# Two modulation products moved behind the experts, one into the end of the RWKV loop, and key factors formed in place

## The chip, the cores and the metric

The kernel runs on one core of a Trainium2 chip. The metric is the device time of one execution in microseconds (us), the median of several runs. TensorE is called PE in the profile (its weight loads PEld), VectorE DVE, ScalarE ACT, GpSimd POOL; SP only issues DMAs.

## The reference, cut to what matters

The block has two layers over 512 latent and 256 context tokens of width 1024 (six tiles of 128 tokens; tiles 0 and 1 are the context). Layer 0 mixes tokens with RWKV-7 heads and S5 groups, layer 1 with latent attention (MLA); each layer ends in a mixture of experts. Both layers are modulated by a vector made from the conditioning:

```
m_l = jnp.split((silu_c @ mod_w[layer] + mod_b[layer])[:, None, :], 6, axis=-1)
m_c = jnp.split(silu_cc @ mod_w[layer] + mod_b[layer], 6, axis=-1)
a_l = modulate(rmsnorm(h_lat, norm1_g[layer]), m_l[0], m_l[1])
...                                   # the layer's mixer gives o_l
h_lat = h_lat + m_l[2] * o_l
f_l = modulate(rmsnorm(h_lat, norm2_g[layer]), m_l[3], m_l[4])
h_lat = h_lat + m_l[5] * moe_ffn(f_l, ...)
```

The six vectors of a layer are one product of 1024 by 6144, 25.2 MB of weights for two rows of input.

## The kernel before

**Modulation.** The product is cut into parts `mod_part(l, q)`: part q = 0 gives shift and scale of the first norm, 1 the first gate and the second shift, 2 the second scale and gate. A part loads 8.39 MB as 16 DMAs of 512 KB on SP (tile `mw`, 128 partitions by 4 by 256 columns, three buffers); each load feeds four products of 256 columns, one in each group of 32 columns of the array. They count as eight PE instructions in the profile, since fp32 takes two passes. They add into `psmod`; DVE adds the bias (`mb`) and SP writes the result to DRAM (`mods`), from where the norms read it.

**Stages.** In the front, layer 0's input projection runs (`pwi`, `pkb`, `ptv`, then `pws` of `w_in_s5`) with all three parts of layer 0 between its pieces. Then comes the loop of `rwkv`: s runs over 0 to 5, and each s makes one step of both scan directions. Stage a (`rwkv_stage_a`) forms decays and key factors on DVE, ACT and POOL (`plo`, `sg`, `ev`, `KB`, `wseg`) two steps ahead. Stage b solves a triangular system one step ahead: DVE makes `X`, SP stores it (`xo`) and loads it as blocks (`D`), and PE with DVE and ACT turns it into an inverse (`pd`, `W`, `G`, `pt`, `Tb`). The steps use it (`pU`, `VU`, `pY`, `pZ`, then the state `Z`). `rwkv_out` makes a token tile's output (`yo`), for tiles 0 and 1 in s = 3, for two more in each of s = 4 and 5. `MODN` puts layer 1's three parts into s = 3, 4 and 5. After the loop come the output projection (`po`) and the experts of layer 0, 768 tokens, whose results (`yo`) go to a DRAM buffer (`yb`).

**MLA stage.** POOL gathers the experts' rows (`cy<-yb`), DVE and POOL combine them into `h`, and SP stores the four latent tiles (`hbuf`). Each tile is normed and transposed (`ntt`), projected (`pmi`), normed and transposed again (`pmt`), and expanded (`pv`). Then attention starts (`pqp`, then `pqn`, `st`).

**What sets the order.** A scheduler simulates the kernel at build time and writes every engine's instructions in one order; on the chip each engine takes them strictly in that order, and a buffer's next user waits for its last reader.

Of the kernel before, what the change touches and what calls it, by code (L numbers as in the profile page):

```python
# [21 lines left out]
OP = mybir.AluOpType  # L22
# [25 lines left out]
MODN = {3: (0,), 4: (1,), 5: (2,)}  # L48
# [39 lines left out]
class Block:  # L88
# [35 lines left out]
    def cond(self, tp):  # L124
        nc, i = self.nc, self.i
        cr = tp.tile([16, 128], F32, name="cr")
        nc.sync.dma_start(cr[0:8, :], i["c"].rearrange("b (k p) -> (b k) p", p=128))
        nc.sync.dma_start(cr[8:16, :], i["c_ctx"].rearrange("(k p) -> k p", p=128))
        cs = tp.tile([16, 128], F32, name="csil")
        nc.scalar.activation(cs, cr, AF.Tanh, scale=0.5)  # L130
        nc.vector.tensor_scalar(cs, cs, 0.5, 0.5, op0=OP.mult, op1=OP.add)
        nc.vector.tensor_tensor(cs, cs, cr, OP.mult)
        pt = self.psum("tp", "pt_c", 2)
        nc.tensor.transpose(pt[:, :16], cs, self.ident[:16, :16])
        self.cst = self.c0.tile([128, 8, 32], F32, name="cst")
        nc.gpsimd.memset(self.cst, 0.0)
        nc.vector.tensor_copy(self.cst[:, :, 0:2], pt[:, :16].rearrange("p (v k) -> p k v", v=2))

    def mod_part(self, l, q, wpool, spool, tag="mod"):
# [18 lines left out]
        for k in range(8):  # L158
            for h in range(2):
                wt = wpool.tile([128, 4, 256], F32, name=f"mw{l}{q}{k}{h}", tag="mw")  # L160
                w = i["mod_w"][l, k * 128:(k + 1) * 128, q * 2048:q * 2048 + 2048].rearrange("p (j c) -> p j c", j=4)
                last = nc.sync.dma_start(wt, w[:, :, 256 * h:256 * h + 256])
                for j in range(4):
                    nc.tensor.matmul(ps[32 * j:32 * j + 32, 256 * h:256 * h + 256], self.cst[:, k, :], wt[:, j],  # L164
                                     start=(k == 0 and h == 0), stop=(k == 7), skip_group_check=True)
# [311 lines left out]
    def rwkv_stage_a(self, s, sp, wp, tag=("gr",), bufs=2):  # L477
# [3 lines left out]
        for z in range(2):  # L481
# [952 lines left out]
    def row_psum(self, rows, name):  # L1434

        out = [self.psum("cb", f"{name}{hf}", 2) for hf in range(2)]
# [178 lines left out]
    def mla_values(self, t):  # L1615

        nc = self.nc
        ts = slice(t * 128, t * 128 + 128)
        for hh in range(2):
            hs = slice(hh * 8, hh * 8 + 8)  # L1620
            ps = self.psum("ca", f"pv{t}{hh}", 2)
            self.mm3(ps, (self.kvT[0][:, ts], self.kvT[1][:, ts]), [x[:, hs, :].rearrange("p h c -> p (h c)") for x in self.kw],
                     True, True)
            dst, src = self.vv[:, t, hs], ps.rearrange("p (h c) -> p h c", h=8)
            if hh:
                nc.vector.tensor_copy(dst, src)
            else:
                nc.scalar.activation(dst, src, AF.Copy)

    def mla_down(self, aT, t, sp):  # L1630
# [12 lines left out]
        pt = self.psum("cb", f"pmt{t}", 2)  # L1643
        if t >= 2:
            r = self.rstd_of(sp, ps[:, 0:256], f"mq{t}", 256)
            qn = sp.tile([128, 256], F32, name=f"qn{t}", tag="qn", bufs=2)
            nc.vector.scalar_tensor_tensor(qn, ps[:, 0:256], r, self.qnb, op0=OP.mult, op1=OP.mult)
            for k in range(2):
                nc.tensor.transpose(pt[:, k * 128:(k + 1) * 128], qn[:, k::2], self.ident)
        r = self.rstd_of(sp, ps[:, 256:384], f"mk{t}", 128)  # L1650
        kn = sp.tile([128, 128], F32, name=f"kn{t}", tag="kn", bufs=2)
        nc.vector.scalar_tensor_tensor(kn, ps[:, 256:384], r, self.kvb, op0=OP.mult, op1=OP.mult)
# [175 lines left out]
    def front(self, qd, es):  # L1828
# [5 lines left out]
        with ExitStack() as e0:  # L1834
# [33 lines left out]
            self.mod_part(0, 2, mp, ms)  # L1868
# [17 lines left out]
    def rwkv(self, es, s5d, rwd):  # L1886
# [25 lines left out]
        for s in range(6):  # L1912
# [47 lines left out]
    def build(self):  # L1960
# [7 lines left out]
        with ExitStack() as es:  # L1968
# [10 lines left out]
            with ExitStack() as ec:  # L1979
# [7 lines left out]
                 lambda: self.mla_weights(self.pool("mlaw", 1, es=mes, side="right")))  # L1987
        with ExitStack() as e0:
# [9 lines left out]
            with ExitStack() as e1:  # L1998
# [5 lines left out]
                for v in (1, 0):  # L2004
                    for hf, ps in enumerate(self.row_psum(self.g2r[:, v], f"g2c{v}")):
                        nc.scalar.activation(g2c[v][:, hf * 512:hf * 512 + 512], ps, AF.Copy)
                self.mla_split(wp)

                def normed(t):
                    h = hts[t]  # L2010
                    self.combine(self.fetch(0, t, xp, 2), h, g2c[int(t < 2)],
# [3 lines left out]
                    r = self.rstd_of(xp, h, f"n1{t}")  # L2015
# [151 lines left out]
```

## Time and profile before

| | us |
|---|---|
| median of three runs | 1959.4 |
| lowest, highest | 1953.17, 1964.0 |
| profiled execution, its own time | 1948.41 |
| its span in the trace | 1946.6 |
| PE busy | 1563.9 (80%) |
| DVE busy | 1218.9 (63%) |
| ACT, POOL busy | 774.2, 701.3 |

The profiled execution took 1.8 us more than its span, and 11 us less than the median. Its mean granted clock of PE is 0.88 of full speed. Stages in the trace: front to about 330 us, loop to 874, output projection and experts to 1268, MLA stage before attention to 1378.

### The profile page before, as it was taken

The numbers are of one execution on the slowest core, as the hardware profiler recorded it, in microseconds if no ns is written. First come the engines' busy times: TensorE is split into PE (matmuls) and PEld (weight loads), VectorE is DVE, ScalarE is ACT, GpSimd is POOL, SyncE is SP. The second block draws the span as 40 slices with busy tenths as digits, with TensorE's granted clock in tenths as the row PEclk, the third lists the DMA queues.
The fourth block names the chain that finished last, engine by engine and source line by source line (L and its number), as shares of the span: only waits on it lengthen the run. The fifth ranks groups of instructions, "written<-read, shape, count | busy, mean of one in ns | idle before, by whom it ended". The sixth has DMA issues, their size and how long they took to land. (4 is left out here: it accounts for less than half of the span.)

```text
span 1946.6 us, 32507 instructions
## 1 busy us (share of the span) xinstructions
PE 1563.9 (80%) x12531; PEld 1126.9 (58%) x12531; DVE 1218.9 (63%) x2385; ACT 774.2 (40%) x1434; POOL 701.3 (36%) x700
## 2 busy tenths in 40 slices
PE   5698898558687789649698999949699998789993
PEld 2376767447576655337575666638455556666662
DVE  4799933884866867243754654475678854575544
ACT  4222324334543523132413555433556543335542
POOL 0476802441423414102514233451143353324432
PEclk8688999678898869679899999969799998899997
DMA  8754587723233268743605999852000009349965
GB/s 257 213 174 157 164 275 218 218 60 109 62 88 103 72 223 258 241 170 128 246 33 188 389 354 367 328 175 65 1 1 1 1 0 367 110 168 370 377 230 184
DMA packets 222854, 347.65 MB, mean 179 GB/s; under 512 B 49538, under 2 KB 170296, under 8 KB 207784
## 3 DMA queue, kind: packets, MB, share of 16 engines
q1 hardware_dynamic: 206784, 294.71, 45.4%
q0 software_dynamic: 10080, 44.04, 6.3%
q10 hardware_dynamic: 5832, 6.78, 1.1%
q8 instruction: 100, 1.64, 0.3%
q14 instruction: 58, 0.48, 0.1%
HBM read 279.02 MB, written 66.46 MB: 177 GB/s over the span
## 5 line engine op out<-in xcount | busy, mean ns | idle before, releaser
L164 PE MATMUL psmod<-mw,cst 128*32 128x256 f32 x768 | 83.8, 491 | 43.5 <-DMA mw<-in_mod_w_dram 39.2
L191 PE MATMUL pwi<-aT,wih 128*128 128x256 f32 (+1 forms) x224 | 81.7, 367 | 14.4 <-DVE q L334 7.2
L192 PE MATMUL pwi<-aT,wih 128*128 128x256 f32 (+1 forms) x224 | 81.9, 367 | 0.0
L193 PE MATMUL pwi<-aT,wil 128*128 128x512 f32 (+1 forms) x224 | 81.2, 364 | 0.0
L1784 ACT ACTIVATE P<-st 128x512 f32<-128x512 f32 x96 | 56.9, 596 | 48.7 <-PE st L1782 44.7
L1797 POOL TENSOR_TENSOR sum<-sum,P 128x512 f32<-128x512 f32 x48 | 63.6, 1348 | 27.8 <-ACT P L1784 27.6
L1112 PE MATMUL s5y<-s5tq,s5H 128*96 128x128 f32 x256 | 50.6, 333 | 27.3 <-POOL s5H L1104 15.1
L1415 POOL DMA_INDIRECT xg<-fbuf,rk x36 | 37.8, 1051 | 92.9 <-PE ptx L231 52.3
L572 PE MATMUL pg<-PQ,KB 64*128 64x128 f32 x384 | 54.1, 318 | 18.7 <-ACT ta L501 10.4
L1098 POOL TENSOR_TENSOR s5t<-s5G,s5tq 128x384 f32<-128x384 f32 x16 | 18.0, 1123 | 141.5 <-DVE s5G L1095 121.3
L185 ACT ACTIVATE xT<-ptx 128x512 fp32r<-128x512 f32 x72 | 41.2, 596 | 66.1 <-PE ptx L231 65.0
L164 PEld LDWEIGHTS psmod<-mw,cst 128*32 128x32 f32 x768 | 20.3, 124 | 77.4 <-DMA mw<-in_mod_w_dram 55.7
L186 DVE TENSOR_TENSOR xT<-ptx,xT 128x512 fp32r<-128x512 f32 x72 | 48.2, 688 | 23.1 <-ACT xT L185 22.2
L572 PEld LDWEIGHTS pg<-PQ,KB 64*128 64x128 f32 x384 | 44.1, 211 | 31.2 <-ACT ta L501 10.7
L191 PEld LDWEIGHTS pwi<-aT,wih 128*128 128x128 f32 x224 | 46.2, 208 | 22.3 <-issue 11.4
L1112 PEld LDWEIGHTS s5y<-s5tq,s5H 128*96 128x96 f32 x256 | 37.8, 198 | 35.9 <-POOL s5H L1104 16.8
L1795 POOL TENSOR_TENSOR sum<-P,P 128x512 f32<-128x512 f32 x16 | 20.5, 1300 | 105.3 <-ACT P L1784 105.2
L231 PEld LDWEIGHTS ptx<-ident,xg 128*128 128x128 f32 x288 | 40.6, 192 | 26.6 <-issue 21.0
L1788 PE MATMUL po<-P,vv 128*64 128x512 f32 x192 | 54.3, 617 | 1.1 <-ACT P L1784 1.1
L685 PE MATMUL pU<-Z,PQ 128*64 128x128 f32 x192 | 30.3, 331 | 27.9 <-ACT Z L677 27.7
L231 PE MATMUL ptx<-ident,xg 128*128 128x128 f32 x288 | 42.9, 285 | 10.9 <-issue 7.0
L192 PEld LDWEIGHTS pwi<-aT,wih 128*128 128x128 f32 x224 | 46.1, 206 | 7.8 <-issue 3.1
(1569 smaller groups left out, 5161.0 us busy)
## 6 DMA issues: line engine op xcount, KB each, us to landing
mw<-in_mod_w_dram SPq DMA_DIRECT2D x96, 512.0 KB
yb<-yo SPq DMA_DIRECT2D x36, 512.0 KB
s5tq<-s5t SPq DMA_DIRECT2D x16, 960.0 KB
yb<-zrow SPq DMA_DIRECT2D x16, 512.0 KB
wi<-in_hy_w_in_dram SPq DMA_DIRECT2D x14, 512.0 KB
rk<-qbuf SPq DMA_DIRECT2D x12, 512.0 KB
fbuf<-f SPq DMA_DIRECT2D x10, 512.0 KB
s5t<-s5CP SPq DMA_DIRECT2D x4, 1152.0 KB
```

Source lines behind the costliest of these rows:

```text
L164: nc.tensor.matmul(ps[32 * j:32 * j + 32, 256 * h:256 * h + 256], self.cst[:, k, :], wt[:, j], start=(k == 0 and h == 0), stop=(k == 7), s ...
L185: nc.scalar.activation(hi, src, AF.Copy)
L186: nc.vector.tensor_tensor(lo, src, hi.bitcast(F32), OP.subtract)
L191: nc.tensor.matmul(out, lh, rh, start=start, stop=False, **kw)
L192: nc.tensor.matmul(out, lh, rl, start=False, stop=False, **kw)
L193: nc.tensor.matmul(out, ll, rh, start=False, stop=stop, **kw)
L231: nc.tensor.transpose(pt[:, k * 128:(k + 1) * 128], a[:, h * 4 + k::8], self.ident)
L572: nc.tensor.matmul(pg[hp][:, m], KB[rs, m, ps2], PQ[rs, m, ps2], start=True, stop=True, skip_group_check=True)
L1112: nc.tensor.matmul(out, H[:, g, d, k, h0:h0 + 96], CP[:, k, d, i0:i0 + 8, :].rearrange("p a b -> p (a b)"), start=False, stop=(d == 1 and ...
L1784: ex = nc.scalar.activation(P, st, AF.Exp, scale=SCALE)
L1788: mm = nc.tensor.matmul(po[64 * x:64 * x + 64], vv[:, kt, h0 + x, :], P, start=(kt == 0), stop=(kt == 5), skip_group_check=True)
L1797: nc.gpsimd.tensor_tensor(sums[x], sums[x], P, OP.add)
```

## The change

`MODN` now holds part (0, 2) in s = 3 and part (1, 0) in s = 4. Parts (1, 1) and (1, 2) stand in the MLA stage behind the experts of layer 0, with 128 columns for each load: 64 loads of 256 KB in four buffers, and half as long products. They have their own accumulator bank `md`, for which `pv`, `pmt` and `g2c` share the three buffers of tag `cb`. `rwkv_out` of tiles 0 and 1 moves to s = 4, behind that step's own tiles. The key factors are written straight to their strided places in `KB`, so `ev` is no longer written a second time in stage a. Three squares for norms are written to tiles that exist anyway (left out below).

```
-MODN = {3: (0,), 4: (1,), 5: (2,)}
+MODN = {3: ((0, 2),), 4: ((1, 0),)}
...
-    def mod_part(self, l, q, wpool, spool, tag="mod"):
+    def mod_part(self, l, q, wpool, spool, tag="mod", parts=2, bufs=None):
...
-            for h in range(2):
-                wt = wpool.tile([128, 4, 256], F32, name=f"mw{l}{q}{k}{h}", tag="mw")
+            for h in range(parts):
+                n = 512 // parts
+                wt = wpool.tile([128, 4, n], F32, name=f"mw{l}{q}{k}{h}", tag="mw", bufs=bufs)
...
-            t1 = ev
             for m in range(4):
-                nc.scalar.activation(t1[:, m, :], ta[:, m, :], AF.Identity, scale=self.hka[:, 0, m:m + 1],
+                nc.scalar.activation(ends(KB)[:, m], spl(ta)[:, m], AF.Identity, scale=self.hka[:, 0, m:m + 1],
                                      bias=self.hka[:, 1, m:m + 1])
-            nc.gpsimd.tensor_tensor(t1, t1, k, OP.mult)
-            nc.vector.tensor_tensor(ends(KB), spl(t1), e3, OP.mult)
+            nc.gpsimd.tensor_tensor(ends(KB), ends(KB), spl(k), OP.mult)
+            nc.vector.tensor_tensor(ends(KB), ends(KB), e3, OP.mult)
...
-            ps = self.psum("ca", f"pv{t}{hh}", 2)
+            ps = self.psum("cb", f"pv{t}{hh}", 3)
...
-            self.mod_part(0, 2, mp, ms)
             self.s5_quad(3, w5)
...
-            if s == 3:
+            if s > 3:
+                ends = {ZT[z][s]: self.rwkv_out(ZT[z][s], op, rwd if s < 5 else None, yy[z]) for z in range(2)}
+            if s == 4:
                 for t in (0, 1):
                     self.rwkv_out(t, op, rwd)
-            elif s > 3:
-                ends = {ZT[z][s]: self.rwkv_out(ZT[z][s], op, rwd if s < 5 else None, yy[z]) for z in range(2)}
             if s in MODN:
-                for q in MODN[s]:
-                    self.mod_part(1, q, mp, ms, MODT)
+                for l, q in MODN[s]:
+                    self.mod_part(l, q, mp, ms, MODT)
...
+        self.ppes.close()
+        self.psum_pool(None, "ppm")
...
                 self.mla_split(wp)
+                for q in (1, 2):
+                    self.mod_part(1, q, mp, mp, "md", 4, 4)
```

Lines of the changed kernel are 2 to 10 higher than before. Here is what stands on PE **at the front's end before**: the first `plo` of stage a, in the row below, has 163 rows behind it since the first `pws` (row 859), psmod's among them.

```order
1017 L191 MATMUL pws_3086<-aT_83,wsh_3081 128x384
1018 L192 MATMUL pws_3086<-aT_83,wsh_3081 128x384
1019 L193 MATMUL pws_3086<-aT_82,wsl_3082 128x384
1021 L192 MATMUL pws_3086<-aT_83,wsh_3081 128x384
1022 L496 MATMUL plo_2767<-q_2765,wu 128x128 x2
1023 L496 MATMUL plo_2768<-q_2765,wu 128x128 x2
```

And **now**: the first `pws` is row 845, the last row 1046.

```order
893 L195 MATMUL pws_2803<-aT_83,wsh_2772 128x384
894 L196 MATMUL pws_2803<-aT_82,wsl_2773 128x384
895 L196 MATMUL pws_2844<-aT_82,wsl_2840 128x384
896 L499 MATMUL plo_2659<-q_2657,wu 128x128
897 L499 MATMUL plo_2660<-q_2657,wu 128x128
```

So `plo` has moved from row 163 of that stretch to row 51, and the 16 loads' psmod rows are gone from it. On SP the loads of `wu`, which `plo` reads, moved ahead too (row 141 to row 92), as did the writes of zeros to `yb` (rows 146 to 156 before, 101 to 107 now).

PE **at the loop's end, s = 5, before** (the blocks `D`, the inverse `pd`, `pt`):

```order
2283 L616 MATMUL pd_8466<-Ta_8399,G_8253 32x32 x32
2284 L616 MATMUL pd_8466<-Ta_8399,G_8299 32x32 x32
2285 L1142 MATMUL s5gl_7830<-s5zT_7811,s5glu 128x512
2286 L164 MATMUL psmod_9168<-mw_9175,cst 32x256 x4
2287 L164 MATMUL psmod_9168<-mw_9181,cst 32x256 x4
2288 L164 MATMUL psmod_9168<-mw_9187,cst 32x256 x4
2289 L620 MATMUL pd_8532<-D_2729,W_2730 32x32 x64
2290 L164 MATMUL psmod_9168<-mw_9193,cst 32x256 x4
2291 L164 MATMUL psmod_9168<-mw_9199,cst 32x256 x4
2292 L164 MATMUL psmod_9168<-mw_9205,cst 32x256 x4
2293 L632 MATMUL pt_8606<-ident,G_8253 32x32 x16
```

and **now** (L164 has become L167, L616 L618, L632 L634, L637 L639):

```order
2300 L167 MATMUL psmod_8680<-mw_8771,cst 32x256 x4
2301 L614 MATMUL pd_8217<-ident,D_2621 32x32
...
2309 L618 MATMUL pd_8283<-Ta_8216,G_8070 32x32 x32
2310 L618 MATMUL pd_8283<-Ta_8216,G_8116 32x32 x32
2311 L1138 MATMUL s5zt_7704<-ident,zt_6709 128x96 x4
2312 L622 MATMUL pd_8349<-D_2621,W_2622 32x32 x64
2313 L1138 MATMUL s5zt_7710<-ident,zt_6709 128x96 x4
2314 L634 MATMUL pt_8423<-ident,G_8070 32x32 x16
...
2316 L1144 MATMUL s5gl_7717<-s5zT_7703,s5glu 128x256
2317 L639 MATMUL pt_8458<-Tb_8422,G_8070 32x32 x16
```

The last psmod of the loop now stands ahead of the first `pd` of s = 5, and none between `pd` and the end of the steps; before, all 16 loads of the last part stood there. On DVE the operations of `rwkv_out` of tiles 0 and 1 now stand between the last row of `X` and the first product `G` of that inverse.

PE **in the MLA stage now**, its last rows before attention (of 64 loads, 12 stand before the first `ntt`, 29 in ones to threes among the tiles' products, and 23 here):

```order
3801 L194 MATMUL pmi_13031<-mwi_11979,aTm_12935 128x416
3802 L167 MATMUL psmod_12221<-mw_12276,cst_11921 32x128 x4
3803 L167 MATMUL psmod_12221<-mw_12282,cst_11921 32x128 x4
...
3806 L194 MATMUL pv_13021<-kwv_11982,kvT_11935 128x512
...
3812 L195 MATMUL pmi_13031<-mwi_11980,aTm_12935 128x416
...
3814 L167 MATMUL psmod_12221<-mw_12300,cst_11921 32x128 x4
...
3826 L1671 MATMUL pmt_13057<-ident,kpe_13085 32x128
3827 L167 MATMUL psmod_12221<-mw_12360,cst_11921 32x128 x4
...
3830 L194 MATMUL pv_13101<-kwv_11982,kvT_11935 128x512
...
3836 L167 MATMUL psmod_12221<-mw_12378,cst_11921 32x128 x4
...
3841 L167 MATMUL psmod_12221<-mw_12408,cst_11921 32x128 x4
3842 L194 MATMUL pqp_13189<-qT_11933,qwp_13181 128x512
```

Before, the same `pv`, `pmt` and `pmi` stood here alone. On **SP** the loads stand among the four writes of `h`; before, those four stood there alone:

```order
485 L165 DMA mw_12125<-in_mod_w_dram 128x4x128
486 L2024 DMA hbuf<-h_9065 128x1024
487 L165 DMA mw_12131<-in_mod_w_dram 128x4x128
...
491 L165 DMA mw_12155<-in_mod_w_dram 128x4x128
492 L2024 DMA hbuf<-h_9066 128x1024
...
502 L2024 DMA hbuf<-h_9068 128x1024
503 L165 DMA mw_12222<-in_mod_w_dram 128x4x128
...
507 L174 DMA mods_8670<-mb_12012 4x512 x2
...
509 L150 DMA mb_12212<-in_mod_b_dram 4x512 x2
...
511 L165 DMA mw_12258<-in_mod_w_dram 128x4x128
```

Of the 64 loads, 32 stand behind the last write of `h`, 27 of these behind the write of the first part's result (row 507, `mods`) as well.

## Rows read from the trace of the kernel before

**Rows 1.** The page, its first line.

```profile
span 1946.6 us, 32507 instructions
```

**Rows 2.** The page, costliest groups: busy us, mean ns | idle before, releaser.

```profile
L164 PE MATMUL psmod<-mw,cst 128*32 128x256 f32 x768 | 83.8, 491 | 43.5 <-DMA mw<-in_mod_w_dram 39.2
```

**Rows 3.** Windows, tile psmod alone: length, busy us (count) PE, PEld, DVE; PEclk.

```profile
200.00:300.00 100.00, 11.59 (x112) 3.05 (x112) 0.00 (x0) 0.97 0.75 232
...
300.00:400.00 100.00, 1.28 (x16) 0.32 (x16) 0.69 (x1) 0.81 0.71 200
...
800.00:900.00 100.00, 12.17 (x120) 3.17 (x120) 0.69 (x1) 0.76 0.60 203
```

**Rows 4.** Windows, all work: busy us PE, PEld, DVE, ACT, POOL; PEclk, DMA share.

```profile
300.00:310.00 10.00, 10.00 (x63) 9.34 (x63) 1.23 (x1) 1.93 (x3) 0.00 (x0) 1.00 0.89 259
...
330.00:340.00 10.00, 2.92 (x24) 2.48 (x22) 8.80 (x11) 9.86 (x28) 4.62 (x3) 0.83 0.95 285
```

**Rows 5.** Waits of PE from 690 to 900 us.

```profile
PE psmod L164 <- DMA mw<-in_mod_w_dram: 18.6, 13, 6.1
```

**Rows 6.** MLA stage: PE's waits; tile hbuf, first and last issue; attention's first product.

```profile
PE ntt L301 <- issue: 24.8, 1, 24.8
...
L2014 SPq DMA_DIRECT2D hbuf<-h x4: 319/323/326, 1299.7 to 1320.6; - x4
...
1377.66 0.76 PE L191 MATMUL pqp<-qT,qwp 128*128 128x512 f32 x1 [0.83 <-ACT ngm L1687]
```

**Rows 7.** Windows of the MLA stage, all work.

```profile
1280.00:1290.00 10.00, 0.00 (x0) 0.00 (x0) 8.45 (x21) 2.98 (x5) 5.44 (x3) 0.50 0.59 188
...
1300.00:1310.00 10.00, 7.97 (x32) 7.71 (x32) 8.84 (x17) 2.37 (x6) 8.61 (x7) 0.53 0.66 227
...
1301.00:1378.00 77.00, 66.34 (x297) 58.34 (x298) 49.03 (x161) 24.97 (x79) 18.60 (x16) 0.88 0.22 73
```

**Rows 8.** Front: timeline of PE, and PE's waits (us, times, longest).

```profile
322.14 1.17 PE L496 MATMUL plo<-q,wu 64*128 64x128 f32 x16
...
PE plo L496 <- DMA q<-q2d: 14.1, 1, 14.1
```

**Rows 9.** Waits of ACT from 300 to 900 us.

```profile
ACT ev L544 <- DVE wseg L519: 39.0, 7, 13.7
```

**Rows 10.** Loop's end, timelines of ACT, DVE, PE: start, us, instructions [idle before].

```profile
804.86 0.47 ACT L617 ACTIVATE W<-pd,odd 128x256 f32<-128x256 f32 x1 [1.09 <-PE pd L616]
...
821.25 1.19 ACT L634 ACTIVATE Tb<-pt 32x512 f32<-32x512 f32 x2 [14.65 <-PE pt L632]
...
829.58 1.29 ACT L645 ACTIVATE G<-pt 32x256 f32<-32x256 f32 x4 [2.70 <-PE pt L642]
...
837.81 1.21 ACT L699 ACTIVATE VU<-pU 64x512 f32<-64x512 f32 x2 [6.94 <-PE pU L697]
...
810.13 3.07 DVE L624 TENSOR_TENSOR G<-D,pd 32x256 f32<-32x256 f32 x8 [2.04 <-PE pd L620]
...
819.28 1.92 PE L632 MATMUL pt<-ident,G 32*32 32x32 f32 x64
...
835.80 1.97 PE L697 MATMUL pU<-R,G 64*64 64x64 f32 x30
...
841.13 1.20 PE L704 MATMUL pZ<-VU,KT 128*64 128x64 f32 x32
...
844.98 0.32 PE L685 MATMUL pU<-Z,PQ 128*64 128x128 f32 x1 [1.72 <-ACT Z L677]
```

**Rows 11.** Timeline of DVE in s = 3, one operation of rwkv_out.

```profile
724.04 0.68 DVE L776 TENSOR_TENSOR yo<-yo,vo 128x512 f32<-128x512 f32 x1
```

**Rows 12.** Lines by form: the products of 128 columns nearest to the new ones.

```profile
L1027 PE MATMUL s5tap<-s5CP,s5bd 128*32 128x128 f32 x128 | 12.9, 279 | 3.7 <-DVE s5CP L808 1.9 <-DVE s5CP L805 1.8
```

**Rows 13.** DMA: 325 to 350 us, then 1273 to 1330 us.

```profile
DMA packets 13791, 6.95 MB, mean 278 GB/s; under 512 B 254, under 2 KB 13786, under 8 KB 13791
...
DMA packets 2740, 10.58 MB, mean 186 GB/s; under 512 B 310, under 2 KB 434, under 8 KB 2610
```

More of the change, by code (lines that the diff above doesn't have):

```diff
@@ L136, in cond @@
         nc.gpsimd.memset(self.cst, 0.0)
-        nc.vector.tensor_copy(self.cst[:, :, 0:2], pt[:, :16].rearrange("p (v k) -> p k v", v=2))
-    def mod_part(self, l, q, wpool, spool, tag="mod"):
+        self.cs2 = self.cp.tile([128, 8, 2], F32, name="cst2")
+        nc.vector.tensor_copy(self.cs2, pt[:, :16].rearrange("p (v k) -> p k v", v=2))
+        nc.vector.tensor_copy(self.cst[:, :, 0:2], self.cs2)
+    def mod_part(self, l, q, wpool, spool, tag="mod", parts=2, bufs=None):
         nc, i = self.nc, self.i
@@ L158, in mod_part @@
         for k in range(8):
-            for h in range(2):
-                wt = wpool.tile([128, 4, 256], F32, name=f"mw{l}{q}{k}{h}", tag="mw")
+            for h in range(parts):
+                n = 512 // parts
+                wt = wpool.tile([128, 4, n], F32, name=f"mw{l}{q}{k}{h}", tag="mw", bufs=bufs)
                 w = i["mod_w"][l, k * 128:(k + 1) * 128, q * 2048:q * 2048 + 2048].rearrange("p (j c) -> p j c", j=4)
-                last = nc.sync.dma_start(wt, w[:, :, 256 * h:256 * h + 256])
+                last = nc.sync.dma_start(wt, w[:, :, n * h:n * h + n])
                 for j in range(4):
-                    nc.tensor.matmul(ps[32 * j:32 * j + 32, 256 * h:256 * h + 256], self.cst[:, k, :], wt[:, j],
+                    nc.tensor.matmul(ps[32 * j:32 * j + 32, n * h:n * h + n], self.cst[:, k, :], wt[:, j],
                                      start=(k == 0 and h == 0), stop=(k == 7), skip_group_check=True)
@@ L1432, in expert_mm, with row_psum @@
         return hh
-    def row_psum(self, rows, name):
-        out = [self.psum("cb", f"{name}{hf}", 2) for hf in range(2)]
+    def row_psum(self, rows, name, tag="cb", bufs=2):
+        out = [self.psum(tag, f"{name}{hf}", bufs) for hf in range(2)]
         for j in range(8):
@@ L1642, in mla_down @@
                 self.mm3(ps[:, 0:416], (aT[0][:, k], aT[1][:, k]), (self.mwi[0][:, k], self.mwi[1][:, k]), False, k == 7)
-        pt = self.psum("cb", f"pmt{t}", 2)
+        pt = self.psum("cb", f"pmt{t}", 3)
         if t >= 2:
-            r = self.rstd_of(sp, ps[:, 0:256], f"mq{t}", 256)
             qn = sp.tile([128, 256], F32, name=f"qn{t}", tag="qn", bufs=2)
+            r = self.rstd_of(sp, ps[:, 0:256], f"mq{t}", 256, sq=qn)
             nc.vector.scalar_tensor_tensor(qn, ps[:, 0:256], r, self.qnb, op0=OP.mult, op1=OP.mult)
@@ L1649, in mla_down @@
                 nc.tensor.transpose(pt[:, k * 128:(k + 1) * 128], qn[:, k::2], self.ident)
-        r = self.rstd_of(sp, ps[:, 256:384], f"mk{t}", 128)
         kn = sp.tile([128, 128], F32, name=f"kn{t}", tag="kn", bufs=2)
+        r = self.rstd_of(sp, ps[:, 256:384], f"mk{t}", 128, sq=kn)
         nc.vector.scalar_tensor_tensor(kn, ps[:, 256:384], r, self.kvb, op0=OP.mult, op1=OP.mult)
@@ L1987, in build @@
                  lambda: self.mla_weights(self.pool("mlaw", 1, es=mes, side="right")))
+        mp = self.pool("mwp2", 1, es=mes, side="right")
+        self.cst = mp.tile([128, 8, 32], F32, name="cst1")
+        nc.gpsimd.memset(self.cst, 0.0)
+        nc.vector.tensor_copy(self.cst[:, :, 0:2], self.cs2)
+        self.ppes.close()
+        self.psum_pool(None, "ppm")
         with ExitStack() as e0:
@@ L2004, in build @@
                 for v in (1, 0):
-                    for hf, ps in enumerate(self.row_psum(self.g2r[:, v], f"g2c{v}")):
+                    for hf, ps in enumerate(self.row_psum(self.g2r[:, v], f"g2c{v}", "cb", 3)):
                         nc.scalar.activation(g2c[v][:, hf * 512:hf * 512 + 512], ps, AF.Copy)
                 self.mla_split(wp)
+                for q in (1, 2):
+                    self.mod_part(1, q, mp, mp, "md", 4, 4)
                 def normed(t):
                     h = hts[t]
-                    self.combine(self.fetch(0, t, xp, 2), h, g2c[int(t < 2)],
+                    ys = self.fetch(0, t, xp, 2)
+                    self.combine(ys, h, g2c[int(t < 2)],
                                  (nc.vector, nc.vector if t < 2 else nc.gpsimd))
@@ L2014, in normed @@
                         nc.sync.dma_start(self.hb[(t - 2) * 128:(t - 1) * 128], h)
-                    r = self.rstd_of(xp, h, f"n1{t}")
+                    r = self.rstd_of(xp, h, f"n1{t}", sq=ys[1])
                     return self.norm_tile(h, r, t, self.mc1, xp)
```

## The prediction

> **What bounds the kernel now.** I read the page's first line and its costliest groups, then windows of psmod alone and of all work, then the waits and timelines at the four places that the change touches. The profiled execution took 1948.41 us, a span of 1946.6 [rows 1] and 1.8 around it. The sum below is made against it; the median of the runs shown, 1959.4, is 11.0 us above it, and I carry the difference over unchanged. No engine bounds the whole kernel. Each stage has a chain of its own, and what matters is whether psmod stands in it.
>
> psmod is the costliest group of the page: 83.8 us of PE for six parts, 14.0 each, and 43.5 us of idle time ahead of it [rows 2]. In the front, part (0, 2) takes 11.59 + 1.28 = 12.9 us (112 + 16 = 128 instructions) [rows 3]. PE is busy without a gap there at full clock (10.00 of 10 us, clock 1.00), while DVE has 1.23 us to do; from 330 us on it is the other way round, DVE 8.80 and PE 2.92 [rows 4]. So up to about 322 us PE alone decides when stage a can begin, and behind it DVE does. At the loop's end PE waits 18.6 us for the weights of psmod, once for 6.1 us [rows 5]. In the MLA stage PE idles 24.8 us before the first transposes [rows 6], with DVE at 8.45 of 10 and the clock at 0.50 [rows 7]; from 1301 to 1378 it is busy 66.34 of 77 us, more than any other engine [rows 7]. The DMA queues are about 0.6 busy in the gap and 0.22 behind it [rows 7].
>
> **Front, part (0, 2) removed.** 12.9 us of PE's work stands in the stretch that PE bounds, so all of it comes off. A second gain is that `plo` now stands 112 rows earlier and that `wu` and the zero writes have moved ahead on SP; before, `plo` came at 322.14 us and a later `plo` waited 14.1 us for `q`, a DMA [rows 8]. Whether this helps depends on DVE, which has 1.2 of every 10 us to spare behind 330 us, so I take 3 us of the 14.1. Bounds: 6 us, if half of it turns into a wait for the inputs of stage a (the 14.1 us show that such waits exist), and 12.9 + 14.1 = 27. Taken: **-16**.
>
> **Loop, middle.** s = 3 and 4 keep one part each, (0, 2) and (1, 0) for (1, 0) and (1, 1); equal work, counted at nothing. The key factors no longer overwrite `ev`, which made ACT wait for `wseg` 39.0 us in seven waits [rows 9]. What `ev` feeds on DVE, the product for `KB`, stands later in DVE's own stream, so most of this wait is hidden. Bounds: a fifth of it on the path, 8 us, and nothing, or a loss of 3 if the strided writes make ACT, POOL and DVE half a microsecond slower in each of six stages a. Taken: **-2**.
>
> **Loop's end, part (1, 2) removed.** Its psmod stands inside the last inverse and the last steps. From `W` to the next step's `pU` the trace has 804.86 to 844.98 us [rows 10]. The chain without psmod, from the durations in [rows 10]: `W` 0.47, the `pd` behind it as long as a `pt` at most, 1.92, `G` 3.07, three `pt` of 1.92 each with two copies `Tb` of 1.19, `G` 1.29, `pU` 1.97, `VU` 1.21, `pZ` 1.20, and from `pZ`'s end to the next `pU` 844.98 - 842.33 = 2.65. That is 21.9 us, so the second step would start at 826.8, 18.2 us earlier. Bounds: psmod's own 12.2 us behind 800 us [rows 3], and those with all 18.6 us of waits, 30.8. The chain is what decides, less a microsecond for the two DMAs of `D` that wait as before. `rwkv_out` of tiles 0 and 1 now has to run on DVE between `X` and `G`; there it has the time in which `xo` is stored and `D` loaded, and I count it at nothing. Two tiles are some 20 operations of 0.68 us [rows 11], about 14 us of DVE; without the cover they would fall on the path, which is a rival below. Taken: **-17**.
>
> **MLA stage, two parts added.** 64 loads, 512 PE instructions. No row shows a product of this form with 128 columns. From below: half a 256-column load at full clock, 12.9 / 16 / 2 = 0.40 us [rows 3]. From above: eight instructions at the 0.10 us that 128 columns take in the `s5tap` group (12.9 us for 128) [rows 12], 0.81 us. I take 0.40, since the four groups side by side are the same. Twelve loads lie in the 24.8 us gap and cost nothing; without the gap they would cost 5 us. The other 52 take 21 us (42 from above) in a stage in which PE has 77 - 66.3 = 10.7 us free. About 7 of these can be filled, which leaves 14.
>
> Then the loads. The nearest rows for 512-byte runs are those of 325 to 350 us: 13791 packets of 504 bytes on average at 278 GB/s [rows 13]. At this rate 256 KB take 0.94 us, and 60 loads take 57 us, in a stretch of 105 us that already moves 10.6 MB (38 us at the same rate) [rows 13]. It fits, but not at its end: 32 loads stand behind the last `hbuf` write (1320.6 us) [rows 6] and the last 23 stand almost back to back on PE before `pqp` (1377.66 us) [rows 6]. Four are loaded ahead, 19 come at 0.94 us, 18 us in place of the 8 that PE needs for them: 10 us, of which some four overlap with the `pv` and `pmt` between them. That adds 6. The gathers of `cy` share the queues with the new loads and come later by 0 to 8 us, 3 taken, and the first transposes, at clock 0.53 before [rows 7], find PE at work before them and save up to 5, 5 taken. 14 + 6 + 3 - 5 = **+18**; bounds +5 (PE fills every gap, no stall) and +40 (0.81 us per load).
>
> The Trainium skill ("DMA: Bandwidth & Descriptors", Measured) asks for at least 1 MiB per DMA, and its fit (Anatomy of one DMA) is about 2.0 us plus the bytes at 436 GB/s: an estimate of 2.6 us for 256 KB, against 3.2 for the 512 KB before. One after another the 64 loads would take 166 us by that and the stage would be some 60 us longer; four in flight bring it to 42. The row at 278 GB/s shows many small runs in flight at nearly full rate, so I keep 0.94, and the page speaks for the first rival.
>
> **Sum.** -16 - 2 - 17 + 18 = -17 us: 1931.4 for an execution like the profiled one, 1942.4 for a median like the one shown. A measurement of this kernel tells about 0.5%, 9.8 us, from no change.
>
> **Rivals.**
> 1. *The new loads are limited by their turnaround.* PE takes the products in order, so a late load holds up the tiles' own products. For: four buffers, SP's order with `hbuf` writes between, the gathers. Against: the rate in [rows 13]. At x us per load the 52 loads from 1301 us on are in at 1301 + 52x, some 13 us of tail work follow, and `pqp` was at 1377.7: the stage costs 52x - 64, and with 35 us won elsewhere the net is 52x - 99. From x = 1.71 the gain is under 9.8 us, at 1.90 nothing is left, from 2.09 the kernel is slower by more than 9.8; at 2.3 it is 21 slower, 1980.
> 2. *The loop's end does not gain.* `rwkv_out` of tiles 0 and 1 on DVE (about 14 us) delays the `G` of the last inverse, since DVE keeps its order. Then -17 shrinks to -3, net -3: 1956. Against: DVE waits there for `D` anyway.
> 3. *More comes off.* The front gives 27 (`plo` early, no wait for `q`), the stage costs only 8: net -27 - 2 - 17 + 8 = -38: 1921.
> 4. *The front is not bound by PE.* The transfers of the front take PE's place: they are 0.89 to 0.95 busy there [rows 4]. Half the part's time is then lost to a wait for them and 6 us come off: net -7, 1952.
>
> **How the numbers follow.** My forecast has 0.46, rival 3 0.14, rival 2 0.12, rival 4 0.12, rival 1 0.16 (0.05 about unchanged, 0.11 slower). The forecast's own range, 1930 to 1950, lies mostly under the bound of 1949.6; a tenth of it lies within 0.5%, 0.04. Faster by over 0.5%: 0.42 + 0.14 + 0.05, the share of rivals 2 and 4 in which the other terms make up for it = 0.61. Slower: 0.11 from rival 1, and 0.02 from rival 2 together with a dear MLA stage = 0.13. Within: the rest, 0.26. The range from 1918 to 1968 leaves out the tail of rival 3 and most of rival 1's slower half.
>
> **What the profile of the changed kernel would show.** Front: the first `plo` near 306 us and DVE above 8 of 10 from 315. Loop's end: no wait for `mw` behind the last inverse, and the second step's first `pU` about 36 us before 844.98 (16 from the front, 2 and 18). MLA stage: psmod of 128 columns at about 0.40 us per load at full clock, 12 loads in the old gap, waits for `mw` of some 5 to 10 us in front of `pqp`, and `pqp` 18 us later relative to the end of the experts. The prediction is wrong if the waits for `mw` there pass 40 us, if `G` waits for `yo` on DVE, or if the front's gain is eaten by a wait for `q` or `rk`.

## The result and the profile after

The changed kernel takes 1983.4 us (median of four runs, 1982.46 to 1988.93) against 1957.1 for the kernel before in the same runs: a ratio of 1.0145, 95% interval 1.0115 to 1.0175. That is 28 us slower by the ratio, 26 between the medians, where 17 less were forecast. The page of its profiled execution begins so, and its psmod group has a second form (the 128 columns):

```profile
span 1980.8 us, 33093 instructions
...
L167 PE MATMUL psmod<-mw,cst 128*32 128x256 f32 (+1 forms) x1024 | 84.0, 404 | 44.4 <-DMA mw<-in_mod_w_dram 39.4
```

psmod's time and its waits are the same as before [rows 2]; they stand elsewhere. The rows of this table divide the 34 us between the two spans (the traced execution of the kernel before was 9 us faster than its median here, the changed one's 1 us, so some 8 of the 34 are no effect of the change):

| starts at (us) | before | after | difference |
|---|---|---|---|
| first `pws` / first `plo` | 290.7 / 322.1 | 304.2 / 315.1 | +13.5 / -7.0 |
| first `xo` | 407.1 | 412.1 | +5.0 |
| last `X` of s = 5 (DVE) | 781.2 | 799.6 | +18.4 |
| first `po` (end of the loop) | 878.4 | 878.7 | +0.3 |
| last expert product of layer 0 | 1267.7 | 1272.7 | +5.0 |
| first `pqp` | 1377.7 | 1409.4 | +31.7 |

**Front.** SP's and ACT's timelines before:

```profile
276.29 0.38 SPq L1045 DMA_DIRECT2D s5t<-s5WT  x1
...
324.55 17.22 SPq L1207 DMA_DIRECT2D yb<-zrow  x11
341.86 1.74 SPq L490 DMA_DIRECT2D q<-q2d  x1
...
286.43 2.01 ACT L185 ACTIVATE wsh<-ws 128x1024 fp32r<-128x1024 f32 x2
```

and after, with PE's wait:

```profile
274.62 1.09 ACT L1037 ACTIVATE s5WT<-s5wt 128x512 f32<-128x512 f32 x2 [1.07 <-PE s5wt L1036]
...
275.63 19.49 SPq L1209 DMA_DIRECT2D yb<-zrow  x11
295.22 1.97 SPq L1047 DMA_DIRECT2D s5t<-s5WT  x1
...
303.11 2.00 ACT L188 ACTIVATE wsh<-ws 128x1024 fp32r<-128x1024 f32 x2 [21.20 <-DMA s5t<-s5WT]
...
PE pws L194 <- ACT wsh L188: 23.4, 1, 23.4
```

Eleven writes of zeros hold SP for 19.49 us. Behind them stands the store of `s5WT`, which ACT had ready at 275.7; `wsh` waits for this store, and PE for `wsh`. From 281 to 304 us PE does nothing; before, it was busy for all 23 us of this stretch. The writes held SP for 17.22 us before too, but later, where a load of `q` stood behind them: the 14.1 us that `plo` waited for `q` [rows 8] end with this load.

**Loop.** The first `xo` is 5 us late, the last row of `X` 18.4, the end of the loop 0.3. So behind `X` 18 us are won, and ahead of it as much is lost, 13 of it in the loop.

**MLA stage.** PE's waits from 1268 to 1412 us, the writes of `h`, SP's last loads, and the tail on PE:

```profile
PE psmod L167 <- DMA mw<-in_mod_w_dram: 16.4, 18, 3.4
...
L2024 SPq DMA_DIRECT2D hbuf<-h x4: 338/418/497, 1308.8 to 1356.4; - x4
...
1367.06 34.58 SPq L165 DMA_DIRECT2D mw<-in_mod_w_dram  x27
...
1385.06 0.43 PE L167 MATMUL psmod<-mw,cst 128*32 128x128 f32 x8 [1.82 <-DMA mw<-in_mod_w_dram]
1385.83 0.43 PE L167 MATMUL psmod<-mw,cst 128*32 128x128 f32 x8 [0.34 <-DMA mw<-in_mod_w_dram]
...
1403.69 0.51 PE L167 MATMUL psmod<-mw,cst 128*32 128x128 f32 x8 [2.40 <-DMA mw<-in_mod_w_dram]
...
1409.43 0.79 PE L194 MATMUL pqp<-qT,qwp 128*128 128x512 f32 x1 [4.33 <-ACT qwp L188]
```

The last write of `h`, 1320.6 before [rows 6], comes at 1356.4; the last 27 loads take 34.58 us, one every 1.28, and PE meets them one by one. The stage takes 136.7 us from the last expert product to `pqp`, 110.0 before.

### The profile page after: what moved, and what is told of

Its sections match the earlier page's. It is cut to its first block, busy times and chain, and to the rows that moved or that the text cites. A ratio compares the mean times of both kernels' runs of the same rounds, so it can differ in the third digit from the quotient of the medians.

```text
span 1980.8 us, 33093 instructions
## 1 busy us (share of the span) xinstructions
PE 1601.9 (81%) x12787; PEld 1159.4 (59%) x12787; DVE 1219.1 (62%) x2387; ACT 771.2 (39%) x1432; POOL 706.7 (36%) x701
## 5 line engine op out<-in xcount | busy, mean ns | idle before, releaser
L167 PE MATMUL psmod<-mw,cst 128*32 128x256 f32 (+1 forms) x1024 | 84.0, 404 | 44.4 <-DMA mw<-in_mod_w_dram 39.4
L574 PE MATMUL pg<-PQ,KB 64*128 64x128 f32 x384 | 59.9, 374 | 29.6 <-DVE KB L552 19.4
L196 PE MATMUL pwi<-aT,wil 128*128 128x256 f32 (+1 forms) x224 | 80.7, 361 | 0.0
L167 PEld LDWEIGHTS psmod<-mw,cst 128*32 128x32 f32 x1024 | 26.2, 121 | 83.7 <-DMA mw<-in_mod_w_dram 61.1
L1799 POOL TENSOR_TENSOR sum<-sum,P 128x512 f32<-128x512 f32 x48 | 63.6, 1347 | 28.3 <-ACT P L1786 28.1
L574 PEld LDWEIGHTS pg<-PQ,KB 64*128 64x128 f32 x384 | 49.5, 262 | 37.8 <-DVE KB L552 20.6
L1114 PE MATMUL s5y<-s5tq,s5H 128*96 128x128 f32 x256 | 54.6, 347 | 17.5 <-POOL s5H L1104 11.8
L548 POOL TENSOR_TENSOR KB<-KB,rk 128x512 f32<-128x512 f32 x12 | 16.4, 1371 | 96.2 <-issue 59.2
```

The costliest lines, as they stand in the source:

```text
L167: nc.tensor.matmul(ps[32 * j:32 * j + 32, n * h:n * h + n], self.cst[:, k, :], wt[:, j], start=(k == 0 and h == 0), stop=(k == 7), skip_gr ...
L196: nc.tensor.matmul(out, ll, rh, start=False, stop=stop, **kw)
L574: nc.tensor.matmul(pg[hp][:, m], KB[rs, m, ps2], PQ[rs, m, ps2], start=True, stop=True, skip_group_check=True)
L1114: nc.tensor.matmul(out, H[:, g, d, k, h0:h0 + 96], CP[:, k, d, i0:i0 + 8, :].rearrange("p a b -> p (a b)"), start=False, stop=(d == 1 and ...
L1799: nc.gpsimd.tensor_tensor(sums[x], sums[x], P, OP.add)
```

## The experiments

Each ratio is to the kernel before in the same runs. Where values of gates are left out, tokens choose other experts in layer 1, so that only times up to `pqp` are read.

**e1_zero_held**, the changed kernel with the zero writes behind the front's last store on SP:

```
+                self.zat = nc.sync.dma_start(...).ins       # in w_in_s5, the last store of u
...
-                self.zero_blocks(z0, s - 1)
+                with self.tc.issue_after(self.zat):
+                    self.zero_blocks(z0, s - 1)
```

> The changed kernel, with the 16 writes of zeros held behind the last store of `u` on SP, about where they stood before; nothing is left out. Theory Z: the changed kernel loses in the front because the zero writes moved ahead of the store of `s5WT`, whose tile's place `wsh` needs; PE then waits 23.4 us for `wsh`. Without them ahead this wait is under 8 us, `pws` starts before 290 us instead of 304.2, and the kernel takes 10 to 23 us less than the changed one (1960 to 1973). Rival: DVE and the loop's own waits absorb it; then the wait goes but `po` still starts near 878 us and the time stays within 5 us of 1983.

1953.2 us, 0.9984 (0.996 to 1.0008): 30 less than the changed kernel. The first rows of `pws` and of `po`, by tile:

```profile
L194 PE MATMUL pws<-aT,wsh x64: 333/334/443, 281.7 to 318.3; 128*128 128x384 f32 x64
...
L194 PE MATMUL po<-wo000hi,cat x24: 392/398/796, 848.9 to 881.4; 128*128 128x512 f32 x24
```

`pws` starts at 281.7 instead of 304.2, and what is left of PE's wait for `wsh` is this row:

```profile
PE pws L194 <- ACT wsh L188: 0.2, 1, 0.2
```

The loop ends at 848.9 instead of 878.7. Theory Z holds, and more came than the 10 to 23 us that it asked for. The hold also changed the scheduler's order behind it: the first `xo` comes 17 us earlier than in the changed kernel (395.2), so that 17 of the 30 can be the stall, and the rest came in the loop.

**e2_no_mla_parts**, **e3_products_only** and **e4_quarter** take the two parts behind the experts apart:

```
-        for k in range(8):
+        for k in range(8 if not (l == 1 and q > 0) else 0):     # e2
...
-                wt = wpool.tile(...); last = nc.sync.dma_start(wt, ...)
+                if parts == 2 or len(ring) < 4: ...             # e3: load and append to ring
+                else: wt = ring[(k * parts + h) % 4]
...
-                for j in range(4):
+                for j in range(4 if l == 0 or q == 0 else 1):   # e4
```

> The changed kernel without the loads and products of parts (1, 1) and (1, 2); these two results then hold the bias alone. Theory M: the two parts in the MLA stage cost 27 us or more, so the time falls to 1956 or below and `pqp` comes 26 to 30 us earlier than 1409.4. Rival: the stage is slow for another reason in the change (the PSUM tags that `pv`, `pmt` and `g2c` now share, the squares written to other tiles); then it falls by under 15 us.

> The changed kernel with four loads instead of 32 for each of the two parts behind the experts; the other 28 loads' products use the four tiles again, so the products are all there and 56 loads are left out. Theory L (the stage waits for loads, directly and through SP's order, where loads and writes of `h` wait for each other): 15 to 27 us less than the changed kernel, 1956 to 1968. Theory P (PE's own time for the 512 products in a stage that PE fills): 0 to 8 us less, 1975 to 1983.

> The changed kernel with one product for each load of the two parts behind the experts instead of four; three quarters of these products are left out, all 64 loads stay at nearly the same places. Theory L (loads): 0 to 8 us less than the changed kernel, 1975 to 1983. Theory P (PE's time): 15 to 22 us less, 1961 to 1968.

They took 1950.2 (0.9975, 0.9942 to 1.0007), 1994.3 (1.0202, 1.0158 to 1.0246) and 1986.2 us (1.0166, 1.0108 to 1.0223). e3's time alone would speak against both theories; its expert routing behind `pqp` is another, 603 us from `pqp` to the end against 571. The stage tells them apart (last expert product to first `pqp`): 102.6 us without the parts, 111.7 with the products and eight loads, 135.9 with all loads and a quarter of the products, 136.7 with all. e3's and e4's rows:

```profile
L1261 PE MATMUL pdne<-ew_192dn,hTe x8: 592/592/697, 1278.9 to 1282.1; 128*128 128x512 f32 x8
...
L199 PE MATMUL pqp<-qT,qwp x16: 392/400/764, 1393.8 to 1540.9; 128*128 128x512 f32 x16
```

```profile
L1257 PE MATMUL pdne<-ew_192dn,hTe x8: 592/592/697, 1277.4 to 1280.5; 128*128 128x512 f32 x8
...
L195 PE MATMUL pqp<-qT,qwp x16: 393/400/796, 1416.4 to 1561.2; 128*128 128x512 f32 x16
PE psmod L167 <- DMA mw<-in_mod_w_dram: 18.8, 20, 3.4
```

The two parts cost 34 us in the stage, as theory M has it: the products 9 and the 56 loads 25 more. So theory L holds for the stage by e3. By e4 it is not shown: with a quarter of the products psmod still keeps PE busy for 29.40 us of the stage, against 30.11 with all, so this edit took hardly any time from PE. In the windows of the stage, all work and then psmod alone, e3 and the changed kernel compare so, with e4's psmod last:

```profile
1282.10:1393.80 111.70, 92.73 (x858) 78.01 (x857) 77.17 (x242) 38.00 (x104) 32.77 (x27) 0.90 0.34 111
...
1282.10:1393.80 111.70, 17.12 (x512) 15.90 (x512) 1.35 (x2) 0.90 0.34 111
...
1272.70:1409.40 136.70, 111.74 (x858) 77.30 (x856) 71.70 (x237) 37.41 (x99) 36.87 (x31) 0.81 0.64 199
...
1272.70:1409.40 136.70, 30.11 (x512) 12.52 (x512) 1.38 (x2) 0.81 0.64 199
...
1280.50:1416.40 135.90, 29.40 (x128) 11.15 (x128) 1.35 (x2) 0.82 0.65 199
```

The first number behind the length is PE's busy time: 19 of the 25 us are longer busy time of PE with as many instructions, 858 (13 of them psmod's; the mean clock of the stage is 0.81 against 0.90), and 6 are idle time.

**f1_hbuf_act**, **f4_half_bytes** and **g2_one_each**, all with the zero writes held, ask what of the loads it is:

```
-                        nc.sync.dma_start(self.hb[...], h)
+                        nc.scalar.dma_start(self.hb[...], h)            # f1
...
-                nc.sync.dma_start(wt, w[:, :, n * h:n * h + n])
+                nc.sync.dma_start(wt, w[:, 0:2, n * h:n * h + n])       # f4, l = 1, q > 0
...
-MODN = {3: ((0, 2),), 4: ((1, 0),)}
+MODN = {3: ((0, 2),), 4: ((1, 0),), 5: ((1, 1),)}                       # g2
```

> The changed kernel with the zero writes held and the four writes of `h` issued by ACT instead of SP; nothing is left out. Theory Q (the loads wait behind the writes of `h` on SP, and those wait for tiles that PE delays): the time from the last expert product to `pqp` falls from 138.3 us by 10 to 20, and the kernel takes that much less than 1953. Theory B (bandwidth and the turnaround of four buffers): by 0 to 5 us.

> The changed kernel with the zero writes held and 128 KB instead of 256 KB in each of the 64 loads behind the experts (two of the four groups of columns take the others' weights, so half the bytes are left out and all products stay). Theory W (bandwidth: the bytes compete with the gathers and set the pace): the stage falls from 138.3 us by 10 to 15. Theory T (the turnaround of a load in four buffers and PE's order, whatever its size): by 0 to 5.

> The changed kernel with the zero writes held and part (1, 1) back in the loop, in s = 5; only part (1, 2) stands behind the experts. If the cost in the MLA stage goes with the number of loads, the stage (last expert product to `pqp`, 138.3 us) falls by 14 to 18 us; if it comes from the last loads alone, by under 6. At the loop's end the part costs 8 to 18 us, so that the sum is within 8 us of 1953.

1952.4 us (0.9993, 0.9971 to 1.0014), 1940.2 (0.9934, 0.9908 to 0.9959) and 1941.6 (0.9924, 0.9899 to 0.9949). The stage, 138.3 in e1, takes 135.7, 128.2 and 116.1 us. So SP's order with the writes of `h` (theory Q) is worth at most 3 us. Half the bytes are worth 10, at the lower end of theory W. But the last loads come hardly closer with half the bytes, one every 1.15 us instead of 1.28:

```profile
1323.04 32.15 SPq L166 DMA_DIRECT2D mw<-in_mod_w_dram  x28
```

Of the 10 us, 6 are won before the last write of `h` (77.6 us behind the last expert product, 83.7 in e1). Half as many loads and products (g2) are worth 22, more than the 14 to 18 expected and more than f4's 10 and half of the products' 9 give together, 14 to 15. The other 7 seem to go with the number of loads; a single measurement of each stage does not say more. The part that g2 puts back costs 2 us at `po`, not 8 to 18, so that the kernel takes 12 us less than e1, where within 8 was expected.

**b1_key** and **b2_move** make one edit each in the kernel before, **e5_key_back** and **e6_out_back** undo one each in e1, **g1_move_key** has both without the moved parts, and **h1_mods_only** the moved parts without both:

```
-            t1 = ev                                      # b1, g1; e5 and h1 the other way
-                nc.scalar.activation(t1[:, m, :], ta[:, m, :], AF.Identity, ...)
+                nc.scalar.activation(ends(KB)[:, m], spl(ta)[:, m], AF.Identity, ...)
...
-            if s == 3:                                   # b2, g1; e6 and h1 the other way
+            if s == 4:
                 for t in (0, 1):
                     self.rwkv_out(t, op, rwd)
```

> The changed kernel with the zero writes held (as e1_zero_held) and the key factors again made in `ev` as before. Theory K (writing the factors straight into `KB` costs time in s = 0 to 2, since `pg` now waits for `KB`, 18.7 us in three waits): the last state of s = 2 comes 8 to 15 us earlier than in e1_zero_held (602.7) and the kernel takes 5 to 15 us less than its 1953. Rival (the place of `plo` and `pws` in PE's order costs it, the key factors give a little): unchanged or up to 5 us more.

> The changed kernel with the zero writes held and `rwkv_out` of tiles 0 and 1 again in s = 3. Theory O (moving it behind `X` is worth something, since it no longer delays `X` of s = 5): `po` comes 5 to 12 us later than 848.9, and the kernel takes as much more than 1953. Rival (the move is hidden or costs DVE time near the end): within 4 us, or less.

> The kernel before with the key factors written straight into `KB` and nothing else changed. Theory K: 3 to 12 us slower than before, with waits of `pg` for `KB`. The prediction's term: 0 to 8 us faster, 2 at the centre. Rival: no difference.

> The kernel before with `rwkv_out` of tiles 0 and 1 moved to s = 4 and nothing else changed. Theory O2 (DVE's 14 us of `yo` stand ahead of `X` of s = 5 in the kernel before, in the stretch from stage a's last `KB` to the last `X`, 94.5 us): this stretch falls to 80 to 85 us and the kernel takes 8 to 16 us less than before. The prediction's term: nothing, 0 to 3 us either way.

> The kernel before with the moved `rwkv_out`, the key factors written into `KB` and the zero writes held behind the last store of `u`; all six modulation parts stay where they were before. Theory O2 and the gain of 5 us for the factors that their undoing showed: 10 to 20 us less than before, 1936 to 1946, which would be faster than before and than the change. Rival (the factors cost 21 us whatever the order is): 1955 to 1965.

> Of the change only the moved modulation parts (with the zero writes held) and the small edits in the MLA stage; `rwkv_out` of tiles 0 and 1 in s = 3 and the key factors in `ev` as before. If the three edits simply add up, from 1976 with the factors in place and 5 us for these: about 1975 to 1981, so the moved parts themselves cost some 20 us, since the MLA stage loses 30 and front and loop together win about 10. Rival (front and loop's end win the 33 us that were forecast for them): 1950 to 1958.

| parts moved | rwkv_out moved | factors in KB | kernel | us | ratio to before (95%) |
|---|---|---|---|---|---|
| | x | | b2_move | 1931.9 | 0.9874 (0.9824 to 0.9925) |
| | | x | b1_key | 1975.6 | 1.0102 (1.0076 to 1.0128) |
| | x | x | g1_move_key | 1956.4 | 1.0015 (0.9996 to 1.0033) |
| x | | | h1_mods_only | 1969.7 | 1.0091 (1.0055 to 1.0127) |
| x | x | | e5_key_back | 1958.0 | 1.0018 (1.0 to 1.0036) |
| x | | x | e6_out_back | 1975.7 | 1.0102 (1.0074 to 1.013) |
| x | x | x | e1_zero_held | 1953.2 | 0.9984 (0.996 to 1.0008) |

All with parts moved, and g1, hold the zero writes. No edit has one price in this table. The parts cost 18 us alone (h1) and 26 with the moved `rwkv_out` (b2 to e5), and nothing where the factors are in `KB` (b1 to e6, g1 to e1). For h1 that is neither the 1975 to 1981 of adding up nor the rival's 1950 to 1958. Theories O and O2 hold, with more than they asked for: the move is worth 22 us in b2, 22 between e6 and e1 and 12 between h1 and e5. In b2 everything up to s = 3 is as before (`xo` 660.9 against 658.2), and the last row of `X`, on DVE, was at 781.19 and is at

```profile
758.57 0.18 DVE L598 TENSOR_TENSOR X<-X,xt 128x15 f32<-128x15 f32 x1
```

From stage a's last `KB` to there the stretch takes 69.1 us in place of 94.5; the 14.6 us of `yo` that DVE did in it are gone, half of S5's operations too (four `s5G` scans of a kind where eight stood), and DVE is busy for 34 us there instead of 68. So the move took more out of the stretch than its own operations. The loop ends 26 us earlier:

```profile
L191 PE MATMUL po<-wo000hi,cat x24: 392/398/796, 852.3 to 886.3; 128*128 128x512 f32 x24
```

Theory K has the sign right for the kernel before, not the size (21 us slower where 3 to 12 were expected; `X` of s = 5 starts its last row at 814.4 and `po` starts at 904.0). It fails for e1, where undoing the factors costs some 5, the rival's case and barely clear of the noise; between h1 and e6 they make no clear difference. g1, slower than b2 by 24, misses the 10 to 20 us that it was to win; it also holds the zero writes, which b2 does not. In b1 the waits of `pg` for `KB` that the theory named are not among the longest; instead DVE reaches stage a's operations for s = 5 some 20 us later, behind those of S5, which stood behind them before. So it is the scheduler's order that the small edit tips. No kernel held the order and changed the edit alone; why it tips so stays open.

**h2_no02** and **h3_no12** leave one part out of b2, **c1_mla** adds the MLA stage's small edits to b2:

```
-        for k in range(8):
+        for k in range(8 if (l, q) != (0, 2) else 0):    # h2; h3: (1, 2)
...
-                    r = self.rstd_of(xp, h, f"n1{t}")
+                    r = self.rstd_of(xp, h, f"n1{t}", sq=ys[1])     # c1, and the tags of pv, pmt, g2c
```

> The kernel b2_move without the loads and products of part (0, 2) (its result is the bias alone), the zero writes held. It shows what the front gives: if PE bounds it as forecast, the first `xo` comes 10 to 16 us before 407.7 and `po` as much before 852.3. Rival (DVE and the loop take it back): the first `xo` comes early, and `po` by less than 6 us.

> The kernel b2_move without the loads and products of part (1, 2) (its result is the bias alone); the order up to the last inverse is the same. It shows what the loop's end gives: as forecast, from the last `X` (758.6) to the last state (818.2) 14 to 18 us less than 59.6, and `po` as much before 852.3. Rival (the chain behind the last `X` has other waits, and the DMAs and DVE at the end take it back): `po` less than 8 us earlier from the last `X`, 93.7 now.

> The kernel b2_move with the small edits of the MLA stage (shared PSUM tags, squares in other tiles, another pool) and all six modulation parts where they were before. The stage without the two parts took 102.6 us from the last expert product to `pqp`, against 110.0 before; if these edits give it, the kernel takes 5 to 9 us less than b2_move, 1923 to 1927; rival: no difference, 1930 to 1934.

h2 and h3 ran once each: 1912.6 and 1917.1 us. In h2 the first `pws` comes 12.9 us earlier than in b2, the first `xo` at 397.8 (407.7 in b2), the last `X` 14 us earlier and `po` at 839.8, 12.5 earlier: the front's gain reaches the end of the loop, as forecast, as far as one trace with an order of its own and the zero writes held can say. In h3 the last state comes 61.8 us behind `X` where it was 59.6 in b2, and `po` 86.9 us behind it where it was 93.7: 7 us, the rival's case.

c1 took 1934.6 (0.9908, 0.9874 to 0.9942), no faster than b2. In its MLA stage, though, the first transposes come 25.4 us behind the last expert product, as early as in e2 (25.8) and 8 us earlier than in b2 (33.2) and before (33.5). First b2, then c1:

```profile
L301 PE MATMUL ntt<-ntd,h x96: 277/402/604, 1277.4 to 1327.8; 128*128 128x128 f32 x96
...
L301 PE MATMUL ntt<-ntd,h x96: 281/402/607, 1281.4 to 1337.2; 128*128 128x128 f32 x96
```

So it is the small edits that shorten this gap in e2; c1 keeps 4 of the 8 us up to `pqp` (107.0 against 111.2), and none in the kernel's time. c1 also shows how far one trace can be trusted. Its order up to `po` is b2's, yet its last state comes 69.5 us behind `X`, not 59.6, and its `po` at 862.3, not 852.3. In between, PE's granted clock differs (the third number from the right), again first b2, then c1:

```profile
790.00:800.00 10.00, 9.60 (x226) 5.22 (x218) 7.83 (x20) 6.08 (x13) 0.00 (x0) 1.00 0.82 264
...
790.00:800.00 10.00, 8.43 (x154) 4.88 (x153) 4.56 (x9) 1.17 (x2) 0.00 (x0) 0.54 0.55 173
```

## Why the prediction was wrong

The forecast was -16 - 2 - 17 + 18; what was measured, step by step:

1. **Front, part (0, 2) removed** (-16). The term was about right for the part alone: 12.5 us at `po` in h2. The step that failed is the sentence that counted the zero writes' new place as a second gain. They went ahead of the store of `s5WT` on SP, and what stands behind them there was not looked up. They are not small: the eleven hold SP for 19.49 us. The trace of before had the sign: the 14.1 us of waiting for `q`, of which the forecast hoped to win 3, stood behind the same writes. The forecast named a wait for `q` or `rk` as what could eat the gain; it was `wsh`, through a store. Holding them back is worth 30 us, which is more than the 28 by which the change is slower. This is the largest single error: without it the change would have come out even (e1).
2. **Loop's middle** (-2). The factors in place cost 21 us by themselves and give 5 in e1. The range given, -8 to +3, did not hold the first. It was worked out from ACT's wait and the durations of the edited operations, while the order on DVE changed with the edit.
3. **`rwkv_out` of tiles 0 and 1** (0). It was asked what the move costs behind `X`, and the answer, nothing, fits b2, where the first `G` comes 25.6 us behind `X` (28.9 before). In the changed kernel DVE goes straight from `rwkv_out`'s `gw` to `G`, 26.5 us behind `X`. In e5 it does so too, and `G` comes at 31.7 where it was 27.6 in h1: there the second rival's delay shows, some 4 us. What the move gives ahead of `X` was not asked: the kernel takes 12 to 22 us less.
4. **Loop's end, part (1, 2) removed** (-17). From the last `X` to the last state the changed kernel takes 55.6 us against 71.8 before, 16 less. h1, which has the parts moved and `rwkv_out` in its old place, takes 56.2 (its last row of `X` and its last state, on DVE):

```profile
786.75 0.18 DVE L601 TENSOR_TENSOR X<-X,xt 128x15 f32<-128x15 f32 x1
...
842.90 1.41 DVE L709 TENSOR_TENSOR Z<-pZ,Z 64x512 f32<-64x512 f32 x2 [8.74 <-PE pZ L707]
```

   So in the order for which the term was worked out it has the right size. It is not the part's worth in every order: in b2, whose `X` comes 23 us earlier than before, this stretch takes 59.6 with the part and 61.8 without (h3), and without it `po` is 7 us nearer to `X`. With c1's 69.5 in b2's own order, these traces do not tell what the part is worth there. And h1 does not keep the gain whole: its first `xo` is 5 us earlier than before, its last `X` 6 later, its `po` 10 earlier.
5. **MLA stage** (+18). +26.7, and 28.3 in e1; 34 above the stage without the parts (e2). The products were put at 14 net and cost 9 alone; the 0.40 us per load at full clock was right (0.43 in the rows above). The 5 us saved before the first transposes came (28.1 us behind the last expert product, 33.5 before), but by the small edits, as c1 shows, not by PE's clock. The term that was mis-sized is the loads': 9 in all (tail and gathers), and they cost 25. The last 27 came one every 1.28 us, not 0.94, and with half the bytes still one every 1.15, so a rate in bytes [rows 13] was the wrong measure. What the waits show is the first rival's mechanism, the turnaround in four buffers: SP waited for buffers that psmod had still to read,

```profile
SPq L165 <- PE psmod L167: 74.2, 41, 11.0
```

   and PE, in its order, for the loads. By the rival's own measure, the 52 loads behind the first transposes took from 1300.8 to 1404.4, when the last one's product started: 2.0 us each, beyond the 1.90 at which it leaves no gain. (Its formula then asks for 40 us. The stage lost 27, since 5 us of work and not 13 stood behind the last load, and the stage itself began 5 us later.) The sign that the forecast gave for it, waits for `mw` of more than 40 us on PE, did not come (16.4): most of the loss shows as PE's longer busy time. The Trainium skill's rule ("DMA: Bandwidth & Descriptors", Measured), 1 MiB per DMA, spoke against the change. The direction agrees: 256 KB every 1.28 us are 205 GB/s, under the 278 of [rows 13]; but no run changes a load's size with the bytes kept, so the rule is not tested. Its fit (Anatomy of one DMA), which the page gives for DMAs issued by GpSimd, would have put four in flight at 42 us and no loss; that is not what the trace shows.

The mod parts together, alone (h1): 18 us slower, `po` 10 us earlier and the stage 28.9 longer. With the zero writes held, the whole change comes out even (e1). Its `po` is then 29.5 us earlier than before, close to the 35 forecast up to there, and that is luck: the parts alone bring 10 of it (h1), the moved `rwkv_out` alone 26 (b2), which the forecast counted at nothing. b2 beats both kernels: 1931.9 us, 22 less than before.

Open: how the 25 us of the loads divide between bytes and turnaround beyond the 10 that f4 shows, why the factors tip the order, and why the loop ahead of `X` takes longer with the parts moved alone. The changed kernel's own order up to `po` was run in four kernels (the change, e2, e3, e4): `po` started at 878.7, 891.8, 888.7 and 886.5, and with b2's order at 852.3 and 862.3 (c1). So a single `po` varies by some 6 us around its mean, and the +0.3 in the first table is at the low end of it; differences of a few us between single traces, as in h3, say little.

## What to carry to other kernels

When work leaves a queue, look at what the scheduler puts in its place: transfers with no due time go forward, and a store that frees a buffer can stand behind them. Hold such transfers behind an instruction of your own.

Ask of a moved step what it frees where it left, not only what it costs where it went: DVE, which takes its instructions in order, had 14.6 us of it ahead of a chain that everything waits for, and the scheduler moved S5's operations with it. And make the edits of a change one at a time; here three edits were worth +18, -22 and +21 alone and, with the zero writes held, nothing together.

## What the runs showed of the hardware

An issue on SP is not always short. Most loads of `mw` in the MLA stage take 0.37 us to issue; eleven writes of 512 KB of zeros, in pieces of 512 bytes, took 19.49 us, 1.77 each on average, with the DMA engines busy throughout (share 1.01 and 1.02 from 280 to 300 us). The store behind them on SP waited for the issues, not for its data, which had been ready for 19 us. The last 27 loads of 256 KB are another case: each issue was short, most 0.37 us again, but one came only every 1.28 us, since SP waited for a buffer in between; the engines were 0.87 busy in the second of these windows:

```profile
290.00:300.00 10.00, 0.00 (x0) 0.00 (x0) 0.00 (x0) 0.00 (x0) 0.00 (x0) 0.50 1.02 289
...
1390.00:1400.00 10.00, 8.18 (x70) 3.54 (x66) 0.72 (x2) 1.26 (x4) 0.00 (x0) 0.50 0.87 255
```

These are the changed kernel's windows (busy us of PE, PEld, DVE, ACT and POOL, clock, DMA share, GB/s): one with every engine idle behind SP's queue, one with PE at half clock among the last loads. There a load's eight instructions took 0.66 us, against 0.43 at full clock a few us earlier.
